# Projections of a two-layer trunk as scaled float16 pairs in place of float32r pairs

## The chip, the cores and the metric

The kernel runs on one core of one Trainium2 chip. The core has five engines that each work through their own queue in order: TensorE (PE, matmuls; its weight loads are shown as PEld), VectorE (DVE), ScalarE (ACT), GpSimd (POOL) and SyncE (SP, which issues most DMAs). The metric is the device time of one execution in microseconds (us).

## What is computed

A trunk of two layers over 2048 latent tokens and 256 context tokens, 1024 wide. The reference, cut to what matters here:

```python
def ab_layer(x, xc, mod, mod_c, w_in, w_out, ...):
    h, gate = adaln(x, mod)                 # rmsnorm(x) * (1 + scale) + shift
    hc, gate_c = adaln(xc, mod_c)
    ... = heads_ab(h @ w_in, *wts)          # splits: cq 256, ckv 256, kr 32, gq 512, gk 128, gv 128, gate 1024
    qa = (rmsnorm(cq, cq_gain) @ w_uq)      # 8 latent heads of 64 + 32
    kv = (rmsnorm(ckv, ckv_gain) @ w_ukv)
    oa = joint_dense_attention(qa, ka, va, kac, vac)
    ob = joint_dense_attention(qb, kb, vb, kbc, vbc)
    mix = concatenate([oa, ob]) * silu(g)
    x = x + gate * (mix @ w_out)            # the same for the context xc

def cd_layer(...):                          # second layer
    ... = heads_cd(h @ w_in, q_gain, k_gain)  # q 512, k 128, v 128, gb 512, gcc 512, gh 512, gate 1024
    oc = joint_window_attention(q, k, v, kc, vc, sink)
    od = gb * short_conv(gcv * gh, conv_w)
    mix = concatenate([oc, od]) * silu(g)
    x = x + gate * (mix @ w_out)
```

## The kernel before

Tokens are worked in 18 tiles of 128: two of context, sixteen of latents. A projection multiplies a tile's normalized tokens, transposed, by weights, over 8 inner blocks of 128. To be near float32, each operand is split into a high and a low part, `hh`, `hl` and `wh`, `wl`, both of type float32r: the high part is a rounding copy by ACT, the low part the difference, by DVE (weights) or POOL (tokens). `mm3` (lines 136 to 143) makes three matmuls per inner block: high by high, high by low, low by high. PE loads the token block as weights for each matmul.

The phases, with their times in the profile:
1. To about 490 us: the modulation of layer 0 is computed (`mod_first`, PE matmuls `pm` over `modw`), weights `wina` (512 columns), `winb` (800) are loaded and split; per tile `x_h` makes `hh`, `hl` (`hf` on DVE, line 244), then `pA` (512 columns), `pB` (288), `pC` (512), and from the latent parts `pq` (2 x 384, weights `wuq`) and `pk` (2 x 512, weights `wkv`); then rope and the transposes of queries and keys (line 559). The framework's scheduler sets the order here. `issue_after` places weight loads behind the modulation's loads on SP's queue.
2. To about 2195 us: attention of 16 heads, in 592 slots (U) whose order is written out by hand (`manual_schedule`, so PE, ACT, DVE and POOL run in that order). A slot has scores (lines 912, 913), exponentials, their split into a float16 pair, and the products with the values (702 to 704); a row maximum for a later block (791, 792) runs ahead. Background steps are spread over slots by `spread(list, first, last)`: `row_steps` (layer 1's modulation), the splits of `wg`, `gate_steps` (`pbg`, lines 682 to 684: per tile and half of the gate 8 steps of three matmuls), the splits of `wo`.
3. To about 2720 us: per tile `stage_a` (silu gate times attention output, transposed and split to `m`), `stage_b` (`py`, two blocks of 512 by `wo`, then residual, line 1057), `stage_c` (`x_h` of layer 1), `stage_d` (`pk` 256 columns, `pq` and `pg` 512 each, the last two for latents only). Weights `w4kv`, `w4q`, `w4g` are loaded and split at the start of this phase, the convolution's `w50` and `w51` near its end.
4. To about 3080 us: the convolution's projections `pz`, 8 blocks of 256 tokens, lines 1198 to 1200, 3072 matmuls of 256 columns.
5. To the end: window attention and the last output projection.

## Time and profile before

| | us |
|---|---|
| median of 3 runs | 3453.53 (3451.55 to 3456.27) |
| the profiled execution | 3457.61 |
| its span from first to last instruction | 3455.7 |
| PE busy | 3299.8 |
| DVE busy | 2326.8 |
| POOL busy | 2042.8 |
| ACT busy | 1752.0 |

In the profile's rows the first number is the start (timeline) or the line of the code, "out<-in" are the program's tile names, x the count. Busy time of PE counts a matmul to its modelled end, so that neighbours overlap; the distance from one start to the next is the pace. Idle time of an engine is shown with the instruction that ended it ("<-"). PEclk is the granted clock of PE as a share of full speed.

### The profile page before, as it was taken

The numbers are of one execution on the slowest core, as the hardware profiler recorded it, in microseconds if no ns is written. First come the engines' busy times: TensorE is split into PE (matmuls) and PEld (weight loads), VectorE is DVE, ScalarE is ACT, GpSimd is POOL, SyncE is SP. The second block draws the span as 40 slices with busy tenths as digits, with TensorE's granted clock in tenths as the row PEclk, the third lists the DMA queues.
The fourth block names the chain that finished last, engine by engine and source line by source line (L and its number), as shares of the span: only waits on it lengthen the run. The fifth ranks groups of instructions, "written<-read, shape, count | busy, mean of one in ns | idle before, by whom it ended". The sixth has DMA issues, their size and how long they took to land. (4 is left out here: it accounts for less than half of the span.)

```text
span 3455.7 us, 75435 instructions
## 1 busy us (share of the span) xinstructions
PE 3299.8 (95%) x30863; PEld 2393.5 (69%) x30863; DVE 2326.8 (67%) x4853; ACT 1752.0 (51%) x2425; POOL 2042.8 (59%) x1590
## 2 busy tenths in 40 slices
PE   8999979999999999999999998799999899989999
PEld 4878744555655555666666664588887899976776
DVE  6888876777777777666766668555555422268886
ACT  4656644666666666666666676422323211033443
POOL 3677745777877787777877777444443211134554
PEclk9999979999999999999999999899999999999999
DMA  6444462112121211111111121444445422253332
GB/s 253 123 135 130 121 187 84 47 48 60 38 58 44 58 53 51 41 54 50 54 38 52 50 82 31 148 136 137 148 142 175 130 65 59 72 154 93 96 104 79
DMA packets 360975, 317.89 MB, mean 92 GB/s; under 512 B 211210, under 2 KB 300122, under 8 KB 360626
## 3 DMA queue, kind: packets, MB, share of 16 engines
q1 hardware_dynamic: 356016, 300.47, 28.6%
q10 hardware_dynamic: 4612, 12.60, 1.2%
q8 instruction: 242, 3.96, 0.5%
q14 instruction: 105, 0.86, 0.1%
HBM read 196.58 MB, written 116.41 MB: 91 GB/s over the span
## 5 line engine op out<-in xcount | busy, mean ns | idle before, releaser
L898 POOL TENSOR_TENSOR Pl<-P,Ph 128x1024 f16<-128x1024 f32 (+1 forms) x592 | 1257.3, 2135 | 438.7 <-DVE Ph L895 212.6
L792 DVE TENSOR_REDUCE part<-mx 128x1 f32<-128x512 f32 x1024 | 687.8, 687 | 372.8 <-PE mx L791 366.5
L702 PE MATMUL av<-v,Ph 128*128 128x65 f16 x5296 | 629.7, 194 | 15.6 <-DVE O L937 11.6
L703 PE MATMUL av<-v,Ph 128*128 128x64 f16 x5296 | 628.8, 195 | 0.0
L704 PE MATMUL av<-v,Pl 128*128 128x65 f16 x5296 | 622.0, 193 | 6.5 <-POOL Pl L898 3.4
L702 PEld LDWEIGHTS <-Ph 128*128 128x128 f16 x5296 | 500.5, 97 | 146.6 <-issue 54.1
L703 PEld LDWEIGHTS <-Ph 128*128 128x128 f16 x5296 | 495.2, 98 | 124.3 <-issue 3.5
L912 PE MATMUL sT<-qh,k 96*128 96x512 f16 (+2 forms) x1776 | 578.2, 380 | 1.7 <-ACT P L915 1.7
L704 PEld LDWEIGHTS <-Pl 128*128 128x128 f16 x5296 | 494.7, 99 | 25.4 <-POOL Pl L1369 12.9
L915 ACT ACTIVATE P<-sT,qsca 128x1024 f32<-128x1024 f32 (+1 forms) x296 | 326.3, 1102 | 336.2 <-PE sT L913 326.6
L913 PE MATMUL sT<-q,k 100*128 100x512 f16 (+2 forms) x1184 | 450.2, 381 | 2.1 <-DVE q L808 2.0
L915 ACT ACTIVATE P<-sT,qscb 128x1024 f32<-128x1024 f32 (+1 forms) x296 | 326.5, 1103 | 247.6 <-PE sT L913 237.9
L791 PE MATMUL mx<-k,qh 96*128 96x512 f16 (+1 forms) x1024 | 396.9, 388 | 33.0 <-DVE part L792 24.9
L897 ACT CAST Ph<-P 128x1024 f16<-128x1024 f32 (+1 forms) x395 | 408.3, 1034 | 11.2
L1369 POOL TENSOR_TENSOR Pl<-P,Ph 128x512 f16<-128x512 f32 x156 | 184.5, 1200 | 157.8 <-DVE Ph L1368 67.9
L912 PEld LDWEIGHTS <-k 96*128 96x128 f16 (+1 forms) x1776 | 155.8, 99 | 111.3 <-issue 9.7
L791 PEld LDWEIGHTS <-qh 96*128 96x128 f16 (+1 forms) x1024 | 100.5, 98 | 141.7 <-issue 83.1
L913 PEld LDWEIGHTS <-k 100*128 100x128 f16 (+1 forms) x1184 | 115.1, 97 | 108.9 <-issue 6.2
L895 DVE CAST Ph<-P 128x1024 f16<-128x1024 f32 (+1 forms) x197 | 153.9, 781 | 8.2 <-ACT P L915 7.1
L1029 POOL TENSOR_TENSOR og<-og 128x1024 f32<-128x1024 f32 x18 | 44.0, 2444 | 174.6 <-ACT og L1028 174.6
L1198 PE MATMUL pz<-hx,w51wg 128*128 128x256 f32 x512 | 143.8, 281 | 0.0
L1199 PE MATMUL pz<-hx,w51wg 128*128 128x256 f32 x512 | 143.5, 280 | 0.0
(441 smaller groups left out, 7989.9 us busy)
## 6 DMA issues: line engine op xcount, KB each, us to landing
bgh<-s_hT SPq DMA_DIRECT2D x36, 512.0 KB, 5.4
xt<-in_x SPq DMA_DIRECT2D x32, 512.0 KB
roww<-in_mod_w SPq DMA_DIRECT2D x64, 256.0 KB, 2.8
hx<-s_h1T SPq DMA_DIRECT2D x32, 512.0 KB, 4.4
s_hT<-hh SPq DMA_DIRECT2D x18, 512.0 KB, 2.6
s_hT<-hl SPq DMA_DIRECT2D x18, 512.0 KB, 2.6
s_Gd<-bgg SPq DMA_DIRECT2D x36, 256.0 KB, 5.0
og<-s_Gd SPq DMA_DIRECT2D x18, 512.0 KB, 6.9
```

The source lines that it names most:

```text
L702: nc.tensor.matmul(o, Ph, v[:, 0:65], start=first, stop=False, skip_group_check=True)
L703: nc.tensor.matmul(o[:, 0:64], Ph, v[:, 66:130], start=False, stop=False, skip_group_check=True)
L704: nc.tensor.matmul(o, Pl, v[:, 0:65], start=False, stop=last, skip_group_check=True)
L791: nc.tensor.matmul(m, q["qh"][0:kk, i * 128:(i + 1) * 128], k1[0:kk, c * 512:(c + 1) * 512], start=True, stop=True)
L792: nc.vector.reduce_max(part[:, i, c:c + 1], m, axis=X)
L895: nc.vector.tensor_copy(hs, ps_)
L897: nc.scalar.copy(hs, ps_)
L898: nc.gpsimd.tensor_tensor(ls, ps_, hs, op=ALU.subtract)
L912: nc.tensor.matmul(s[:, j, :w], kk[0:rows_, ks], q["qh"][0:rows_, :w], start=pi == 0, stop=False)
L913: nc.tensor.matmul(s[:, j, :w], d["last"][0:r2, ks], q["q2"][0:r2, :w], start=False, stop=True)
L915: nc.scalar.activation(P[:, :, :w], s[:, :, :w], AF.Exp, scale=d["sc"][:, 2:3])
L1369: nc.gpsimd.tensor_tensor(Pl, P, Ph, op=ALU.subtract)
```

## The change

All projections but the last output projection take float16 pairs. So that float16's range holds, operands are scaled by powers of two: weights by one scale per weight matrix, found from the largest absolute value (`weights16`: load all rows; `top`, a maximum per row block on DVE; `fin`, which brings the maximum over the partitions by a PE transposition, makes the power of two in `pow2` and spreads it by a PE matmul; `split`, ACT then DVE); tokens by a scale from the modulation (`mod_scale`), which is multiplied into the modulation; the gated attention output by a scale per token. The results are scaled back where they are copied from PSUM, by factors from `inv2`. Raw weights now stay in buffers of their own until the scale is known. In phase 1 the load of `wina` stands ahead of the modulation's loads. In phase 2 the loads of `wg` and `wo` are at slots 1 and 44, their maxima at 8 to 18 and 54 to 64. `hT`, `h1T` and `hx` are half as large. Gate and attention output of `stage_a` are two tiles instead of one.

```diff
-        self.hT = [s(f"hT{i}", (NT, 128, D)) for i in range(2)]
+        self.hT = [s(f"hT{i}", (NT, 128, D), F16) for i in range(2)]
...
+    def pow2_bits(self, e, m, top):
+        nc = self.nc
+        nc.vector.tensor_scalar(e, m.bitcast(I32), 0x7F800000, None, op0=ALU.bitwise_and)
+        nc.vector.tensor_scalar(e, e, float(40 << 23), float(230 << 23), op0=ALU.max, op1=ALU.min)
+        nc.vector.tensor_scalar(e, e, -1.0, float((253 + top) << 23), op0=ALU.mult, op1=ALU.add)
+    def inv_bits(self, o, e):
+        self.nc.vector.tensor_scalar(o, e, -1.0, float(254 << 23), op0=ALU.mult, op1=ALU.add)
+    def pow2(self, ps, tag, m1, top, name):
+        nc, c = self.nc, self.c
+        m = c.tile([1, 1], F32, name=f"pm{name}")
+        e = c.tile([1, 2], I32, name=f"pe{name}")
+        sc = c.tile([128, 2], F32, name=f"pw{name}")
+        pt = ps.tile([128, 512], F32, tag=tag, name="pw")
+        nc.tensor.transpose(pt[0:1, 0:128], m1, self.ident)
+        nc.vector.tensor_reduce(m, pt[0:1, 0:128], axis=X, op=ALU.max)
+        self.pow2_bits(e[:, 0:1], m, top)
+        self.inv_bits(e[:, 1:2], e[:, 0:1])
+        p2 = ps.tile([128, 512], F32, tag=tag, name="pw2")
+        nc.tensor.matmul(p2[:, 0:2], self.ones1, e.bitcast(F32), start=True, stop=True)
+        nc.vector.tensor_copy(sc, p2[:, 0:2])
+        return sc
+    def weights16(self, ps, pstag, name, n, nk, src, rp, rtag, outs, scale=None, chunk=None):
+        nc, c = self.nc, self.c
+        raws, S = [], {}
+        am = c.tile([128, nk], F32, name=f"am{name}")
+        Ws = [[[], []] for _ in outs]
+        chunk = chunk or n
+        def load(k):
+            raw = rp.tile([128, n], F32, tag=f"{rtag}{k}", name=f"{name}r{k}")
+            raws.append(raw)
+            for cs, ap in src(k):
+                dst = raw[:, cs]
...
+                S["dma"] = nc.sync.dma_start(out=dst, in_=ap)
+        def top(k):
+            if scale:
+                nc.vector.tensor_scalar(raws[k], raws[k], scale(k), None, op0=ALU.mult)
+            nc.vector.tensor_reduce(am[:, k:k + 1], raws[k], axis=X, op=ALU.max, apply_absolute_value=True)
+        def fin():
+            m1 = c.tile([128, 1], F32, name=f"am1{name}")
+            nc.vector.tensor_reduce(m1, am, axis=X, op=ALU.max)
+            S["sc"] = self.pow2(ps, pstag, m1, 9, name)
+        def split(k, o, c0):
+            pool, tag, b0, w = outs[o]
+            if c0 == 0:
+                for i in range(2):
+                    Ws[o][i].append(pool.tile([128, w], F16, tag=f"{tag}{i}_{k}", name=f"{name}{o}{i}_{k}"))
+            d = slice(c0, min(w, c0 + chunk))
+            x = slice(b0 + d.start, b0 + d.stop)
+            wh, wl = Ws[o][0][k][:, d], Ws[o][1][k][:, d]
+            nc.scalar.activation(wh, raws[k][:, x], AF.Identity, scale=S["sc"][:, 0:1])
+            nc.vector.scalar_tensor_tensor(wl, raws[k][:, x], S["sc"][:, 0:1], wh, op0=ALU.mult, op1=ALU.subtract)
...
+        return loads, mids, splits, Ws, S
+    def inv2(self, name, a, b, f=None):
+        o = self.c.tile([128, 2], F32, name=f"iv{name}")
+        self.nc.vector.tensor_scalar(o[:, 0:1], a, b, None, op0=ALU.mult)
...
+        return o
+    def mod_scale(self, layer, ps, tag):
+        nc, c = self.nc, self.c
+        m = self.mod[layer]
+        am = c.tile([128, 2], F32, name=f"mam{layer}")
+        for i in range(2):
+            nc.vector.tensor_reduce(am[:, i:i + 1], m[:, i * KD:(i + 1) * KD, :].rearrange("p b j -> p (b j)"), axis=X, op=ALU.max, apply_absolute_value=True)
+        m1 = c.tile([128, 1], F32, name=f"mam1{layer}")
+        nc.vector.tensor_scalar(m1, am[:, 1:2], float(D) ** 0.5, am[:, 0:1], op0=ALU.mult, op1=ALU.add)
+        sc = self.hsc[layer] = self.pow2(ps, tag, m1, 14, f"h{layer}")
+        nc.vector.tensor_scalar(m, m, sc[:, 0:1], None, op0=ALU.mult)
...
-        hh = wp.tile([128, KD, 128], F32R, tag="hh", name="hh", bufs=bufs)
-        hl = wp.tile([128, KD, 128], F32R, tag="hl", name="hl", bufs=bufs)
+        hh = wp.tile([128, KD, 128], F16, tag="hh", name="hh", bufs=bufs)
+        hl = wp.tile([128, KD, 128], F16, tag="hl", name="hl", bufs=bufs)
...
+                la, ma, sa, (wina,), xa = self.weights16(ps, "tr", "wina", 512, KD, self.rows_of(a["ab_w_in"][0], 0, 512), wt, "ra", [(wt, "wina", 0, 512)])
+                lb, mb, sb, (winb,), xb = self.weights16(ps, "tr", "winb", NP1 - 512, KD, self.rows_of(a["ab_w_in"][0], 512, NP1 - 512), wt, "rb",
+                                                         [(wt, "winb", 0, NP1 - 512)])
+                for f in la:
+                    f()
                 self.x_norm(S[tiles[0]]["xt"], gp, sqrt=True)
-                after = self.mod_first(sp, ps, "mm")
+                with tc.issue_after(xa["dma"].ins):
+                    after = self.mod_first(sp, ps, "mm")
+                for f in ma + sa:
+                    f()
+                self.mod_scale(0, ps, "tr")
                 x_tr(tiles[0])
                 with tc.issue_after(after.ins):
-                    sa, wina = self.weights(wt, "wina", 512, KD, self.rows_of(a["ab_w_in"][0], 0, 512))
-                    sb, winb = self.weights(wt, "winb", NP1 - 512, KD, self.rows_of(a["ab_w_in"][0], 512, NP1 - 512),
-                                            sub=lambda k: (nc.vector, nc.gpsimd)[k % 2])
-                    for f in sa + sb:
+                    for f in lb + mb + sb:
                         f()
...
-                nc.scalar.copy(c, pA)
+                nc.scalar.activation(c, pA, AF.Identity, scale=iva)
...
+            lg, mg, sg, (wg,), xg = self.weights16(ps, "mx", "wg", D, KD, self.rows_of(a["ab_w_in"][0], NP1, D), wgp, "wgr", [(wgp, "wg", 0, D)], chunk=512)
+            lo, mo, so, (wo,), xo = self.weights16(ps, "mx", "wo", D, KD, self.rows_of(a["ab_w_out"][0], 0, D), wgp, "wgr", [(wgp, "wg", 0, D)], chunk=512)
             gate = self.gate_steps(sp, hp, ps, wg, 1)
-            so, wo = self.weights(wgp, "wo", D, KD, self.rows_of(a["ab_w_out"][0], 0, D), tag="wg", extra=(hp, "h1"), chunk=512)
...
-            spread([lambda f=f: behind(f) for f in sg], 15, 40)
+            spread([lambda f=f: behind(f) for f in lg], 1, 2)
+            spread(mg + [ivg], 8, 18)
...
-            spread(rows[n0 + nd:], U - 40, U - 2)
+            spread(rows[n0 + nd:], U - 44, U - 6)
+            spread([lambda: self.mod_scale(1, ps, "mx")], U - 4, U - 3)
...
+                am = wp.tile([128, 1], F32, tag="am", name="am", bufs=2)
+                nc.vector.tensor_reduce(am, g, axis=X, op=ALU.max, apply_absolute_value=True)
+                e = wp.tile([128, 2], I32, tag="ae", name="ae", bufs=3)
+                self.pow2_bits(e[:, 0:1], am, 14)
+                self.inv_bits(e[:, 1:2], e[:, 0:1])
+                nc.scalar.activation(g, g, AF.Identity, scale=e.bitcast(F32)[:, 0:1])
+                m = hp.tile([128, 2, KD, 128], F16, tag="h1", name="m")
...
-                    nc.vector.tensor_tensor(x1[:, cs], py, g[:, cs], op=ALU.mult)
+                    nc.vector.scalar_tensor_tensor(x1[:, cs], py, iv, g[:, cs], op0=ALU.mult, op1=ALU.mult)
...
+            todo = []
             for nm, c0, w in (("kv", 512, 256), ("q", 0, 512), ("g", 2304, 512)):
-                ss, W[nm] = self.weights(kvp if nm == "kv" else w4, f"w4{nm}", w, KD, self.rows_of(a["cd_w_in"][0], c0, w), extra=(wp, "sq"))
-                for f in ss:
...
+            for x in todo:
+                for f in x[1]:
                     f()
+            IV = {}
+            for nm, _, mids, splits, (W[nm],), x in todo:
+                for f in mids + splits:
+                    f()
+                IV[nm] = self.inv2(nm, x["sc"][:, 1:2], self.hsc[1][:, 1:2], 0.125)
...
+                    c0 = self.conv_weights(ps, 0, ((1, 2), (0, 3)), wgp, [(w4, "w4q", 0, 512), (w4, "w4g", 512, 512)])
+                    for f in c0[0] + c0[1] + c0[2]:
+                        f()
             self.v_scales(wp, ps)
-            c1, W1 = self.conv_weights(1, (0, 1, 2, 3), wgp, "wg", (wp, "xt"))
-            for f in c1:
+            c1 = self.conv_weights(ps, 1, ((0, 1, 2, 3),), wgp, [(wgp, "wg", 0, D)])
+            for f in c1[0] + c1[1] + c1[2]:
...
-                nc.vector.tensor_tensor(u[:, 2:B + 2], pz[1], tmp, op=ALU.mult)
+                iv = self.ivc[c // 2]
+                nc.scalar.activation(tmp, pz[0], AF.Identity, scale=iv)
+                nc.vector.scalar_tensor_tensor(u[:, 2:B + 2], pz[1], iv, tmp, op0=ALU.mult, op1=ALU.mult)
```

Where the change moves instructions, the engines' queues stand as follows (line numbers of after are those of the changed program).

DVE, phase 1, before the first tile's `hf`. `winar`, `wkvr` and so on are raw weights, `macc` the modulation, `am` maxima, `pe` and `pw` the steps of a scale. Before:

```order
L108 TENSOR_TENSOR wina_5_276<-winar_274,wina_5_275 128x512
L196 TENSOR_TENSOR macc<-macc,pm 2x512
L108 TENSOR_TENSOR wina_6_282<-winar_280,wina_6_281 128x512
L108 TENSOR_TENSOR winb_0_294<-winbr_292,winb_0_293 128x800
L199 COPY mod_73<-prt 128x32
L597 MEMSET von 10x128
L108 TENSOR_TENSOR wina_7_288<-winar_286,wina_7_287 128x512
L244 TENSOR_SCALAR hf<-pt,mod_73 128x128 x8
```

After, the place at which the scale of `wina` is made (its last two steps and copy; the splits of `wina` and then `hf` follow):

```order
L136 TENSOR_SCALAR pewina<-pewina 1x1
L181 TENSOR_REDUCE amwuq<-wuqr_412 128x1
L220 TENSOR_SCALAR mam_295<-mam_292 128x1
L180 TENSOR_SCALAR wkvr_446<-wkvr_446,gcmla_ckv_gain 128x1024
L181 TENSOR_REDUCE amwuq<-wuqr_414 128x1
L137 TENSOR_SCALAR pewina<-pewina 1x1
L180 TENSOR_SCALAR wkvr_448<-wkvr_448,gcmla_ckv_gain 128x1024
L181 TENSOR_REDUCE amwkv<-wkvr_446 128x1
L185 TENSOR_REDUCE am1wuq<-amwuq 128x1
L141 TENSOR_SCALAR pewina<-pewina 1x1
L181 TENSOR_REDUCE amwkv<-wkvr_448 128x1
L156 COPY pwwina<-pw_257 128x2
```

The splits of `wina` stood between the steps of the modulation; now the steps of its scale stand between the scalings and maxima of `wuq` and `wkv`.

PE, the start of phase 1, `prt` the modulation's transposition, `pw` a scale's. Before:

```order
L191 MATMUL pm<-modw,sc 2x512 x32
L198 MATMUL prt<-ident,macc 128x2 x4
L241 MATMUL pt<-ident,xt 128x128 x8
L198 MATMUL prt<-ident,macc 128x2 x12
L241 MATMUL pt<-ident,xt 128x128 x8
L141 MATMUL pA<-wina_0_245,hh 128x512
L142 MATMUL pA<-wina_0_246,hh 128x512
```

After:

```order
L286 MATMUL pm<-modw,sc 2x512 x32
L293 MATMUL prt<-ident,macc 128x2 x4
L150 MATMUL pw<-ident,am1wina 1x128
L293 MATMUL prt<-ident,macc 128x2 x12
L155 MATMUL pw_257<-pewina,ones_72 128x2
L150 MATMUL pw<-ident,mam_295 1x128
L155 MATMUL pw_307<-peh_298,ones_72 128x2
L336 MATMUL pt<-ident,xt 128x128 x8
L150 MATMUL pw<-ident,am1winb 1x128
L233 LDWEIGHTS hh
L233 MATMUL pA<-wina_0_260,hh 128x512
```

Transpositions of `xt` and the first `pA` now stand behind the two scales' transpositions and matmuls.

DVE, the start of phase 3, up to the first product of the output projection (`x<-py`). Before:

```order
L108 TENSOR_TENSOR w4kv_0_34371<-w4kvr_34369,w4kv_0_34370 128x256
L108 TENSOR_TENSOR w4kv_1_34377<-w4kvr_34375,w4kv_1_34376 128x256
L108 TENSOR_TENSOR w4kv_2_34383<-w4kvr_34381,w4kv_2_34382 128x256
L1057 TENSOR_TENSOR x_34275<-py,gbc 128x512
L108 TENSOR_TENSOR w4kv_3_34389<-w4kvr_34387,w4kv_3_34388 128x256
L1058 TENSOR_TENSOR x_34275<-x_34275,xt 128x512
```

After:

```order
L181 TENSOR_REDUCE amw4g<-w4gr_34602 128x1
L181 TENSOR_REDUCE amw4g<-w4gr_34604 128x1
L185 TENSOR_REDUCE am1w4kv<-amw4kv 128x1
L181 TENSOR_REDUCE amw4g<-w4gr_34606 128x1
L181 TENSOR_REDUCE amw4g<-w4gr_34608 128x1
L181 TENSOR_REDUCE amw4g<-w4gr_34610 128x1
L181 TENSOR_REDUCE amw4g<-w4gr_34612 128x1
L181 TENSOR_REDUCE amw4g<-w4gr_34614 128x1
L1143 TENSOR_REDUCE am<-gg 128x1
L181 TENSOR_REDUCE amw4g<-w4gr_34616 128x1
L135 TENSOR_SCALAR ae<-am 128x1
L1177 SCALAR_TENSOR_TENSOR x_34464<-py,ivt,gbc 128x512
```

Three splits of `w4kv` stood ahead of that product; now the maxima of `w4kv` and `w4g` do, and the splits come behind it.

More of the change, by code (lines that the diff above doesn't have):

```diff
@@ L71, in __init__ @@
         self.x1d = s("x1d", (SEQ, D))
-        self.h1T = [s(f"h1T{i}", (NT, 128, D)) for i in range(2)]
+        self.h1T = [s(f"h1T{i}", (NT, 128, D), F16) for i in range(2)]
         self.QT1 = [s(f"QT1{i}", (8 * 64, TOK), F16) for i in range(2)]
@@ new lines, in weights16 @@
+    def weights16(self, ps, pstag, name, n, nk, src, rp, rtag, outs, scale=None, chunk=None):
[9 more added lines that the diff above has]
+                dst = raw[:, cs]
+                if len(ap.shape) == 3:
+                    dst = dst.rearrange("p (s c) -> p s c", s=ap.shape[1])
+                S["dma"] = nc.sync.dma_start(out=dst, in_=ap)
[17 more added lines that the diff above has]
+            nc.vector.scalar_tensor_tensor(wl, raws[k][:, x], S["sc"][:, 0:1], wh, op0=ALU.mult, op1=ALU.subtract)
+        loads = [lambda k=k: load(k) for k in range(nk)]
+        mids = [lambda k=k: top(k) for k in range(nk)] + [fin]
+        splits = [lambda k=k, o=o, c0=c0: split(k, o, c0) for k in range(nk) for o in range(len(outs)) for c0 in range(0, outs[o][3], chunk)]
+        return loads, mids, splits, Ws, S
@@ L1008, in gate_bcast, with phase34 @@
         return out
-    def phase34(self, wo, wgp, hp, w4, tiles=range(NT)):
+    def phase34(self, wo, xo, wgp, hp, w4, tiles=range(NT)):
         nc, tc, a = self.nc, self.tc, self.a
@@ L1147, in phase34 @@
-            for f in c1:
-                f()
-            self.wconv = {(0, s): (W, x) for (_, W), p in zip(pairs, ((1, 2), (0, 3))) for x, s in enumerate(p)}
-            self.wconv.update({(1, s): (W1, s) for s in range(4)})
-    def conv_weights(self, cp, parts, pool, tag, extra=None):
-        runs = {(1, 2): ((0, 2, 1280),), (0, 3): ((0, 1, 768), (1, 1, 2816)), (0, 1, 2, 3): ((0, 3, 768), (3, 1, 2816))}[parts]
+            c1 = self.conv_weights(ps, 1, ((0, 1, 2, 3),), wgp, [(wgp, "wg", 0, D)])
@@ new lines, in phase34, with conv_weights @@
+            for f in c1[0] + c1[1] + c1[2]:
+                f()
+            self.wconv = {(0, s): (W, x) for W, p in zip(c0[3], ((1, 2), (0, 3))) for x, s in enumerate(p)}
+            self.wconv.update({(1, s): (c1[3][0], s) for s in range(4)})
+            self.ivc = [self.inv2(f"c{i}", x[4]["sc"][:, 1:2], self.hsc[1][:, 1:2])[:, 0:1] for i, x in enumerate((c0, c1))]
+    def conv_weights(self, ps, cp, groups, rp, outs):
+        base = (768, 1280, 1792, 2816)
+        order = [p for g in groups for p in g]
@@ L1157, in src @@
         def src(k):
             rows = self.a["cd_w_in"][0, k * 128:(k + 1) * 128, :]
-            return [(slice(x * 256, (x + m) * 256), rows[:, c0:c0 + 512 * m].rearrange("p (s c) -> p s c", c=512)[:, :, cp * 256:cp * 256 + 256])
-                    for x, m, c0 in runs]
-        return self.weights(pool, f"w5{cp}{tag}", 256 * len(parts), KD, src, tag=tag, extra=extra)
+            return [(slice(x * 256, (x + 1) * 256), rows[:, base[p] + cp * 256:base[p] + cp * 256 + 256]) for x, p in enumerate(order)]
@@ L1164, in hx_load @@
+        return self.weights16(ps, "tr", f"w5{cp}", 256 * len(order), KD, src, rp, "wgr", outs, chunk=512)
     def hx_load(self, pool, b):
-        hx = [pool.tile([128, KD, 2, 128], F32R, tag=f"h{i}", name=f"hx{i}", bufs=1) for i in range(2)]
+        hx = [pool.tile([128, KD, 2, 128], F16, tag=f"h{2 + i}", name=f"hx{i}", bufs=1) for i in range(2)]
         for j in range(2):
@@ L1506, in emit @@
         if 3 in phases:
-            P.phase34(wo, wgp, hp, w4)
+            P.phase34(wo, xo, wgp, hp, w4)
         if 4 in phases:
```

101 lines of the change are left out of this document (56 added, 45 removed).

## The prediction

> **What bounds the kernel now.** I read the busy lines of the page first, then busy time in chosen stretches, then the spacing of matmuls in the timeline.
>
> ```profile
> PE 3299.8 (95%) x30863; PEld 2393.5 (69%) x30863; DVE 2326.8 (67%) x4853; ACT 1752.0 (51%) x2425; POOL 2042.8 (59%) x1590
> PE   8999979999999999999999998799999899989999
> DVE  6888876777777777666766668555555422268886
> core 0: us, PE busy (x) PEld busy (x) DVE busy (x) ACT busy (x) POOL busy (x), PEclk, DMA share, GB/s
> 200.00:300.00 100.00, 95.30 (x590) 80.59 (x588) 88.50 (x203) 61.42 (x156) 71.81 (x118) 1.00 0.45 132
> ...
> 600.00:700.00 100.00, 91.23 (x1056) 54.88 (x1055) 76.78 (x120) 63.49 (x67) 70.82 (x34) 0.94 0.16 43
> 1500.00:1700.00 200.00, 199.74 (x2406) 128.87 (x2403) 131.25 (x221) 136.19 (x131) 155.26 (x75) 1.00 0.16 49
> 2100.00:2200.00 100.00, 79.67 (x1003) 49.27 (x1000) 60.92 (x95) 61.09 (x66) 71.43 (x33) 0.90 0.10 29
> 2200.00:2300.00 100.00, 91.88 (x448) 75.06 (x447) 63.91 (x177) 37.70 (x69) 37.38 (x42) 0.93 0.55 193
> 2300.00:2400.00 100.00, 100.00 (x520) 83.28 (x519) 55.40 (x164) 28.16 (x52) 49.53 (x64) 1.00 0.40 138
> ...
> 2800.00:2900.00 100.00, 100.00 (x845) 100.00 (x845) 22.57 (x61) 10.02 (x26) 10.24 (x17) 1.00 0.32 87
> ```
>
> TensorE (PE) carries the time: 95% busy, and 100 of 100 us in the output projections (2300 to 2400) and the convolution's projections (2800 to 2900), nearly that in the attention (1500 to 1700). There a matmul that takes its turn sooner is time won, one for one. In phase 1 (200 to 300) DVE is only 7 us behind PE, so DVE caps what a faster PE wins. At the joints (2100 to 2300) PE already waits.
>
> **What a float16 matmul is worth.** Busy time overlaps, so I take start-to-start distances: float32r 512 columns (pq), float16 512 (scores) and float16 256, 512 and 384 of the window stage, then float32r 256 (pz).
>
> ```profile
> 2269.42 0.40 PE L143 MATMUL pq<-w4q,hl 128*128 128x512 f32 x1
> ...
> 2271.06 0.39 PE L141 MATMUL pq<-w4q,hh 128*128 128x512 f32 x1
> 1502.24 0.38 PE L912 MATMUL sT<-qh,k 128*128 128x512 f16 x1
> ...
> 1503.11 0.38 PE L791 MATMUL mx<-k,qh 128*128 128x512 f16 x1
> 3149.34 0.38 PE L1306 MATMUL pc<-k,qT 128*128 128x256 f16 x2
> 3149.56 0.32 PE L1311 MATMUL pl<-k,qT 128*128 128x384 f16 x1
> 3149.72 0.38 PE L1355 MATMUL sT<-qT,k 128*128 128x512 f16 x1
> 2849.79 0.28 PE L1198 MATMUL pz<-hx,w50w4g 128*128 128x256 f32 x1
> ...
> 2850.38 0.28 PE L1200 MATMUL pz<-hx,w50w4g 128*128 128x256 f32 x1
> ```
>
> Seven float32r steps of 512 take 1.64 us, .2343 each; four float16 steps take .87, .2175 each: .0168 won per matmul. Five float32r steps of 256 take .59, .118 each; the float16 pair takes .22, .110 each: .008 won, or .009 if half of .2175 holds (.1088). Every one of these has a weight load of its own.
>
> In the attention, a projection step of three float32r matmuls stands alone between float16 ones:
>
> ```profile
> 1500.86 0.48 PE L682 MATMUL pbg<-wg,bgh 128*128 128x512 f32 x1
> 1501.17 0.40 PE L683 MATMUL pbg<-wg,bgh 128*128 128x512 f32 x1
> 1501.41 0.40 PE L684 MATMUL pbg<-wg,bgh 128*128 128x512 f32 x1
> 1501.65 0.39 PE L791 MATMUL mx<-k,qh 128*128 128x512 f16 x1
> L682 PE MATMUL pbg<-wg,bgh 128*128 128x512 f32 x288 | 139.3, 484 | 0.0
> L682 PEld LDWEIGHTS pbg<-wg,bgh 128*128 128x128 f32 x288 | 54.8, 190 | 2.1
> L702 PEld LDWEIGHTS <-Ph 128*128 128x128 f16 x5296 | 500.5, 97 | 146.6 <-issue 54.1 <-DVE O L937 19.8 <-DVE Ph L1368 4.4
> ```
>
> It holds PE for .79 us; its first matmul is .07 longer, since a float32 load takes 190 ns and stands behind short matmuls, where a float16 load takes 97. Three float16 matmuls would take .65: .14 won, 288 times.
>
> The page "TensorE: Matmul & The Clock Gate" of the Trainium skill, section "Back-to-back issue gap", gives about 216 ns for an isolated warm 512-column matmul and 131 ns sustained for pairs of load and matmul. The scores' .2175 are such pairs and agree with the first, not the second; what the second would make of the time is the last rival below.
>
> **Gains.** Each count is tiles times column blocks times 8 inner blocks times 3.
> - Gate steps, attention: 288 x .137 = **39 us**, PE-bound there. Without the load effect 864 x .0168 = 15.
> - Phase 3: out projection 18 x 2 x 24 = 864, pq and pg 16 x 2 x 24 = 768, at .0168: 27; pk 432 x .0085 = 4. Minus what the joints don't bind on, **29**.
> - Convolution: 3072 x .0085 = **26** (25 to 28).
> - Phase 1: per tile 60 matmuls of 512 and 36 shorter ones. At the .229 spaced in that stage for pA (below) .0115 x 60 = .7, the 36 others about .4: 1.1 per tile; 16 steady tiles 18 us if PE alone bound. But DVE has 88.5 of each 100 us with work that stays, and PE's own wait is on a chain through ACT:
>
> ```profile
> 187.56 0.51 PE L559 MATMUL pt<-ident,mqh 128*128 128x128 f16 x6 [1.18 <-ACT mqh L547]
> ...
> 307.43 0.51 PE L559 MATMUL pt<-ident,mqh 128*128 128x128 f16 x6 [1.18 <-ACT mqh L547]
> 47.44 0.40 PE L141 MATMUL pA<-wina,hh 128*128 128x512 f32 x1
> ...
> 49.73 0.39 PE L142 MATMUL pA<-wina,hh 128*128 128x512 f32 x1
> ```
>
> Five tiles in 119.87 us, 23.97 each, of it 21.2 for DVE. pA: ten steps in 2.29, .229 each. I take **14** (0 to 20).
>
> Sum 39 + 29 + 26 + 14 = 108.
>
> **What it adds.** At the start the weights' scale must be known before any weight can be split. Before: modulation matmuls from 8.48, then the first pA; DMA feeds the weights behind them.
>
> ```profile
> 8.48 30.56 PE L191 MATMUL pm<-modw,sc 128*2 128x512 f32 x64 [2.88 <-DMA modw<-in_mod_w]
> 24.11 7.83 SPq L126 DMA_DIRECT2D winar<-in_ab_w_in  x8
> 32.26 5.00 ACT L107 CAST wina<-winar 128x512 fp32r<-128x512 f32 x8 [22.49 <-DMA winar<-in_ab_w_in]
> 40.71 0.97 DVE L108 TENSOR_TENSOR winb<-winbr,winb 128x800 fp32r<-128x800 f32 x1
> 42.40 2.62 DVE L244 TENSOR_SCALAR hf<-pt,mod 128x128 f32<-128x128 f32 x8
> 44.45 0.50 PE L141 MATMUL pA<-wina,hh 128*128 128x512 f32 x1
> 69.81 0.39 PE L143 MATMUL pA<-wina,hl 128*128 128x512 f32 x1
> L529 DVE TENSOR_REDUCE v<-sq 128x8 f32<-128x768 f32 x18 | 16.9, 941 | 0.0
> L106 DVE TENSOR_SCALAR wkvr<-wkvr,gcmla_ckv_gain 128x1024 f32<-128x1024 f32 x2 | 2.1, 1051 | 1.2 <-DMA wkvr<-in_mla_w_ukv 1.2
> ```
>
> Now the load of wina (2.1 MB) is issued ahead of the modulation's, so modulation ends some 5 us later, about 44 (8 pieces took 7.8 us to issue). On DVE the small steps of wina's scale stand behind eight maxima of winb (800 wide, .97 by the winb row), four scalings and four maxima of wuq and wkv (.94 to 1.05) and the DMA waits of these: some 16 us of DVE work, and wkv's pieces are the last loads. I put wina's scale at 58 in place of the first cast at 32; then 5 us of casts (the ACT row), whose first piece frees PE, and hf's 2.6 us after the modulation is rescaled: first pA near 65 instead of 44.45. winb's splits again follow their scale, on PE's queue behind pA: 8 x .97 on ACT and DVE. I walked this to the end of tile 1's pA: 88 against 69.81. **Loss 19.** Lower bound 5 (the load alone), upper 26. Phase 1 has no later slack that returns it.
>
> Attention: eight maxima 1024 wide of wg (slots 8 to 18) and of wo (54 to 64). From L529's 941 at 768 I estimate 1.2 us each, 20 us on a DVE with 76.8 of 100 us taken (600 to 700); maxima of the scores queue behind them and PE waits for those. The slots of the two batches last some 60 us, with 14 free: 6 lost. Each scale is a transposition, a maximum, four small steps and a matmul in PE's order, about 2 us in which PE stands at its matmul unless work lies between; wg, wo and the second layer's modulation: 3 us. Late loads of w4q, whose maxima stand in DVE's order by the last slots, behind buffers that wo's splits free: 2. **Loss 11** (3 to 20).
>
> Start of phase 3: eight maxima each for kv and g (.4 to .7) are in DVE's order ahead of the first product of the out projection, and kv, q and g split only after their scales: PE runs out of PSUM tiles and then waits for pk's weights. DVE has about 8 us more, plus three chains of some 2. **Loss 8** (3 to 14). The per-token scale of each tile (a 1024 maximum, four small steps, an ACT pass) lies beside PE's 100 of 100 us, DVE being at 55.4: nothing, at most 1 us a tile if it came late (18). Convolution: c1's loads, eight maxima (9.6 us) and splits start only behind the last tile, but its weights are needed after c0's work, so a loss of 3 (0 to 8). Smaller stores of hT and h1T are hidden: DMA share is .32 to .40.
>
> Losses 19 + 11 + 8 + 3 = 41. Net **-67**. The profiled execution took 3457.61 us (span 3455.7 and 1.9 around it), 4.1 over the median 3453.53; less 67 it gives 3390.6, and from the median 3386.5. I say **3388**.
>
> The same page, section "What's actually happening", has PE drop to half clock after about 3.4 us idle. The profile shows a granted clock of .93 in 2200 to 2300, where PE waits; a start with PE idle from 44 to 65 would by that rule cost some 2 us more, which the bound of 26 holds.
>
> **Rivals.**
> 1. *Small costs.* Chains hide beside other work and start-up costs 10: losses 5 to 15, net -93 to -103, 3350 to 3361. For it: ACT and DVE idle at the joints. Against: in-order queues.
> 2. *DVE becomes the bound.* Phase 1 wins nothing (-14) and the maxima cost their upper ends (26, 20, 14, 8): 94 - 68 = 26 won, 3427. For it: 88.5 in phase 1. Against: each upper end has slack before it.
> 3. *Matmuls aren't faster.* If what makes .234 of .2175 isn't the type but, say, a full 128-row weight in a row of three, only the gate steps' load gap goes: 288 x .07 = 20 won, 41 lost, 21 **slower**: 3475. It decides at the spacing: some 4,900 matmuls of 512 columns in all (256 counted half), so losses outweigh from 21 / 4900 = .0043 won, a float16 spacing above .230. Against: L1355 has 128 x 128 weights in float16 and takes .22.
> 4. *A large stall* that I don't see, at one joint: by a DVE wait for a load that waits for a buffer PE frees. 108 us would have to be lost for no gain, 67 more than I count; against: all idle time of PE, over the whole span, is 156 us today (3455.7 less 3299.8).
> 5. *Closer rows.* If consecutive float16 matmuls overlapped, each hundredth of a us below .2175 would win 49 us more on 4,900 of them; at half of .2175, some 530, about 2860. Against: the spacing of the scores, .2175 over four steps, and of L1355, .22. By the 131 ns of the Trainium skill's page it would be about 2960; no row of the trace bears that out.
>
> **Chances.** Forecast (net -45 to -93) 0.70; small costs 0.09; DVE bound 0.11; not faster 0.06; a large stall 0.03; closer rows 0.01. The range for 8 in 10: 3345 to 3435, with both bounds of the joints. Faster by over 0.2% (7 us, about what a measurement of this kernel can tell from no change) 0.89; within it 0.03; slower 0.08 (the third rival and most of the fourth).
>
> **What would show it.** Starts of consecutive pz matmuls .109 apart and of pq .2175; gate steps .65; first pA near 65 and pA of tile 1 done near 88; phase 1 at about 23.1 a tile; PE waiting for DVE in slots 8 to 18 and 54 to 64 and before the first pk. I am wrong if float16 spacing here exceeds .225, or if PE idle time grows by over 60 us.

## The result, and the profile after

| | before | after |
|---|---|---|
| median, runs side by side (us) | 3454.84 (3451.55 to 3456.27) | 3432.36 (3430.84 to 3434.76) |
| span of the profiled execution (us) | 3455.7 | 3433.0 |
| ratio after / before, 95% interval | | 0.9937 (0.992 to 0.9954) |

About 22 us faster, where 67 were forecast. The page of after, PE's busy time and the two rows of tenths that show its work and its granted clock in 40 slices:

```profile
PE 3205.5 (93%) x30902; PEld 2012.4 (59%) x30902; DVE 2448.2 (71%) x5158; ACT 1811.1 (53%) x2451; POOL 2018.3 (59%) x1586
PE   6999968899999999999999998689999799989999
PEclk8999988999999999999999999889999899989999
```

PE's busy time fell by 94.3 us (from 3299.8), the span by 22.7. So PE stands more: 227.5 us without work instead of 155.9. Busy time in the stretches that were shown of before:

```profile
core 0: us, PE busy (x) PEld busy (x) DVE busy (x) ACT busy (x) POOL busy (x), PEclk, DMA share, GB/s
200.00:300.00 100.00, 92.41 (x605) 53.69 (x604) 86.63 (x204) 68.14 (x162) 76.21 (x123) 1.00 0.41 110
600.00:700.00 100.00, 82.31 (x962) 49.15 (x963) 79.22 (x125) 59.55 (x64) 64.47 (x31) 0.95 0.25 71
2200.00:2300.00 100.00, 72.15 (x347) 38.38 (x348) 76.87 (x220) 37.31 (x60) 26.79 (x27) 0.80 0.55 177
2300.00:2400.00 100.00, 100.00 (x574) 55.28 (x572) 72.45 (x201) 38.56 (x64) 46.52 (x63) 1.00 0.40 135
2800.00:2900.00 100.00, 100.00 (x918) 89.63 (x916) 25.15 (x67) 13.06 (x29) 11.60 (x19) 1.00 0.20 46
```

The steady stages stay full of PE work and hold more matmuls in 100 us (574 for 520, 918 for 845). The joint at 2200 went from 91.88 to 72.15, and its granted clock from .93 to .80. The pace of the float16 pairs, from the timeline of after: the output projection, the convolution, and a gate step between its neighbours.

```profile
2307.67 0.38 PE L233 MATMUL py<-wo,m 128*128 128x512 f16 x1
...
2311.34 0.38 PE L235 MATMUL py<-wo,m 128*128 128x512 f16 x1
2829.81 0.27 PE L1328 MATMUL pz<-hx,w 128*128 128x256 f16 x1
...
2830.90 0.27 PE L1329 MATMUL pz<-hx,w 128*128 128x256 f16 x1
1500.49 0.38 PE L786 MATMUL pbg<-wg,bgh 128*128 128x512 f16 x1
...
1501.14 0.38 PE L895 MATMUL mx<-k,qh 128*128 128x512 f16 x1
```

17 steps in 3.67 us are .216 each (the scores of before gave .2175), ten of 256 columns in 1.09 are .109, and the gate step is .65. All three are as forecast. Where the two timelines drift apart, by the starts of the same instruction in both, in order of the program (minus: after gains on before; the two profiled spans differ by the sum):

| stretch | forecast | measured |
|---|---|---|
| start, to pA of tile 3 | +19 | +21.9 |
| phase 1 on, to pA of tile 17 | -14 | -10.3 |
| end of phase 1, to the scores of slot 0 | 0 | +6.2 |
| slots 0 to 66 | with the next but one +11 | +18.4 |
| slots 66 to 550 (gate steps) | -39 | -33.1 |
| slots 550 to 591 | see above | +4.9 |
| to py of tile 2 (start of phase 3) | +8 | +19.0 |
| py of tile 2 to tile 16 | -29 | -27.0 |
| to pz no. 385 (start of the convolution) | +3 | -2.3 |
| pz no. 385 to the last | -26 | -24.6 |
| to the end | 0 | +4.1 |
| sum | -67 | -22.8 |

(Of the forecast's 29 and 26, two tiles and 384 pz lie in the row "to pz no. 385"; at the pace of their neighbours these win 3.9 and 3.5, so about 5 are lost at that joint.) With them the gains are 102 of the 108 forecast, and the losses 80 instead of 41.

### The profile page after: what moved, and what is told of

It is laid out like the page before. It is cut to its first block, busy times and chain, and to the rows that moved or that the text cites. A ratio compares the mean times of both kernels' runs of the same rounds, so it can differ in the third digit from the quotient of the medians.

```text
span 3433.0 us, 75844 instructions
## 1 busy us (share of the span) xinstructions
PE 3205.5 (93%) x30902; PEld 2012.4 (59%) x30902; DVE 2448.2 (71%) x5158; ACT 1811.1 (53%) x2451; POOL 2018.3 (59%) x1586
## 5 line engine op out<-in xcount | busy, mean ns | idle before, releaser
L1009 ACT CAST Ph<-P 128x1024 f16<-128x1024 f32 (+1 forms) x395 | 407.8, 1032 | 11.3
L1330 PE MATMUL pz<-hx,w 128*128 128x256 f16 x1024 | 278.8, 273 | 5.3 <-DVE w L197 5.0
L1328 PE MATMUL pz<-hx,w 128*128 128x256 f16 x1024 | 279.0, 273 | 1.0 <-ACT tmp L1343 0.9
L1329 PE MATMUL pz<-hx,w 128*128 128x256 f16 x1024 | 278.9, 273 | 0.0
```

The source lines that it names most:

```text
L1009: nc.scalar.copy(hs, ps_)
L1328: nc.tensor.matmul(p[:, 0:B], wh[k][:, cs], hv, start=k == 0, stop=False)
L1329: nc.tensor.matmul(p[:, 0:B], wh[k][:, cs], lv, start=False, stop=False)
```

## The experiments

Two theories at first. A: the losses are the price of finding the scales (maxima, the chain to a power of two and back, waits behind them in in-order queues). B: they are something else of the change, such as later loads, splits of two passes or a joint that a faster PE merely waits at. Four kernels put constants in place of scales, first by phase, then all at once. In this diff the names listed are those of the group; the modulation's and the token's scale are replaced likewise. Powers of two that suit the data are built in, so these kernels show times and are no replacement.

```diff
+            if name not in FIX:
+                nc.vector.tensor_reduce(am[:, k:k + 1], raws[k], axis=X, op=ALU.max, apply_absolute_value=True)
...
+            if name in FIX:
+                S["sc"] = self.fx[FIX[name]]
+                return
```

**Constants in phase 1** (`wina`, `winb`, `wuq`, `wkv`, the modulation of layer 0).

> Leaves out, in phase 1 alone, the finding of scales (maxima, transpositions, power-of-two steps of wina, winb, wuq, wkv and of layer 0's modulation); constants stand in their place, all else is the changed kernel. Theory A (the price is the finding of scales in in-order queues): the first pA starts near 50 us instead of 62.9, pA of tile 1 near 68 instead of 88.1, and the kernel is 14 to 20 us faster than the changed one: 3412 to 3418. Theory B (phase 1 is bound by DVE, ACT and POOL together, so an earlier start is given back by its end): less than 8 us faster, 3424 to 3432, with the first scores of the attention at 525 to 532 instead of 531.8.

3416.26 us, ratio 0.9895 (0.9879 to 0.9911): 16 us under after. At pA of tile 3 the loss is 5.8 instead of 21.9. The first pA is at 54.6 (near 50 was expected), still 10.2 later than before. That part is not the finding of scales; the load of `wina` ahead of the modulation's and the order of the work around it are left for it, and were not taken apart.

**Constants in the attention** (`wg`, `wo`, the modulation of layer 1).

> Leaves out the finding of the scales of wg, wo and of layer 1's modulation in the attention; constants stand in their place. The changed kernel lost 18.9 us against the one before between slots 12 and 66 and 4.7 in the last four slots. Theory A: these come from the maxima and the chains, so 18 to 24 us faster than the changed kernel: 3408 to 3414. Theory B (the splits by ACT and DVE at slots 20 to 40, now reading three operands, are what costs): the loss at slots 12 to 54 stays, some 6 us, and the gain is 11 to 14: 3418 to 3421.

3413.48 us, 0.9884 (0.987 to 0.9899): 19 us under after. Between slots 0 and 66 the kernel loses 1.4 instead of 18.4, and between 550 and 591 nothing.

**Constants in phases 3 and 4** (`w4kv`, `w4q`, `w4g`, `w50`, `w51`, and the scale per token).

> Leaves out the finding of the scales of w4kv, w4q, w4g, w50, w51 and of the per-token scale of the gated attention output (maximum and power of two; the scaling pass of ScalarE stays); constants stand in their place. Theory A: the 19 us lost at the start of phase 3 fall to 5 to 9 and the 6 at the convolution's start to 0 to 3, so 13 to 20 us faster than the changed kernel: 3412 to 3419. Theory B (the order of the loads and the splits, not the scales, sets the start of phase 3): under 6 us faster, 3426 to 3432.

3398.80 us, 0.9849 (0.9833 to 0.9866): 33.6 us under after, more than either theory had. From slot 591 to py of tile 2 it wins 5.9 where after loses 19.0, and some 9 more come at the start of the convolution.

**All constants.**

> All three together: every scale but the last projection's is a constant, so what is left is float16 pairs with splits, scaling passes and rescaling on the way out of PSUM. Theory A: the parts add, 50 to 64 us faster than the changed kernel: 3368 to 3382, some 75 to 85 under the kernel before. Theory B: 15 to 30 us faster, 3402 to 3417.

3364.61 us, 0.9742 (0.9728 to 0.9757): 67.8 us under after; the three parts (16.1, 18.9, 33.6) add to 68.6. So the price of finding scales is about 68 us, spread over separate places, and what is left, the float16 pairs with their splits and scaling passes, wins 89 (3453.27 less 3364.61 in the same runs). Some losses stay: 5.3 to pA of tile 3, 3.6 in the last stage, and 5.9 between the last pC and slot 0. PE's waits at this last place, by groups (line, operation, busy time and mean, then the idle time ahead of them), of before:

```profile
L372 PE MATMUL pt<-ident,gqh 128*128 128x128 f16 x16 | 1.8, 262 | 7.3 <-ACT gqh L358 5.0 <-DVE gqh L359 2.2
L141 PE MATMUL pq<-wuq,ch 128*128 128x384 f32 x4 | 1.4, 362 | 1.4 <-ACT ch L499 1.4
```

and of after:

```profile
L233 PE MATMUL pk<-wkv,ch 128*128 128x512 f16 x4 | 2.0, 506 | 0.0
L467 PE MATMUL pt<-ident,gqh 128*128 128x128 f16 x16 | 1.8, 263 | 9.5 <-ACT gqh L453 7.3 <-DVE gqh L454 2.2
L233 PE MATMUL pq<-wuq,ch 128*128 128x384 f16 x4 | 1.7, 422 | 4.2 <-ACT ch L603 4.2
```

PE is done sooner and waits 5.0 us longer for the same passes of ACT (2.8 for `ch`, 2.3 for `gqh`, by these rows). It then runs the first pk at half clock: four from 483.13 on start .425 apart, which brings the mean of that row to 506 ns where before has 392 to 396. I read this as phase 1's gain handed back in part at its end; the loss is there with and without scales, but no run shows that the earlier end is its cause.

**Order alone.** Two moves: `wina`'s maxima, scale and splits ahead of the modulation in the program; `wo`'s maxima spread over slots 300 to 500 instead of 54 to 64.

```diff
+                for f in ma + sa:
+                    f()
                 with tc.issue_after(xa["dma"].ins):
                     after = self.mod_first(sp, ps, "mm")
-                for f in ma + sa:
-                    f()
...
-            spread(mo, 54, 64)
+            spread(mo, 300, 500)
```

> Two moves, nothing left out. (1) Maxima, scale and splits of wina stand in the program ahead of the modulation's matmuls, so that on PE the scale's transposition and matmul come before the 64 modulation matmuls instead of behind them. Theory A (wina's scale was late since its steps stood behind the modulation on PE and behind winb, wuq and wkv on DVE): first pA 8 us earlier, near 55, as with constants (54.6), and pA of tile 3 near 120 instead of 131.9. Theory B (winb's scale and splits and the token path set the start anyway): first pA earlier, but pA of tile 3 within 3 us of 131.9. (2) The maxima and scale of wo at slots 300 to 500 instead of 54 to 64. Theory A (eight maxima of 1.2 us stand in DVE's order where DVE has no time left): of the 12.7 us lost between slots 54 and 66 at least 9 are won, and little is lost at slots 300 to 500, where DVE is 66 to 70% busy. Theory B (the scale's chain, in which PE waits, is the price): 3 us or less are won. Both A: 3408 to 3414; both B: 3427 to 3432.

3415.08 us, 0.9894 (0.9879 to 0.9909): 17 us under after. Two thirds of it are `wo`: slots 54 to 66 win 2.0 instead of losing 12.5, and after the maxima at their new place 11.3 of the 14.5 are left at slot 591. Most of the rest is the start (pA of tile 3 at 127.3 instead of 131.9). Slots 54 to 66 of before, of the changed kernel, of the kernel further down that has only the token's scale as a constant (its code up to here is the changed kernel's), and of this one (PE busy, PEld, DVE, ACT, POOL, then the granted clock):

```profile
695.80:732.00 36.20, 34.28 (x402) 20.57 (x399) 29.60 (x48) 21.68 (x21) 25.94 (x13) 0.95 0.19 47
719.40:768.20 48.80, 41.38 (x406) 23.05 (x403) 38.74 (x63) 21.71 (x21) 25.71 (x13) 0.83 0.14 35
720.40:763.10 42.70, 33.83 (x406) 19.91 (x403) 38.94 (x63) 21.72 (x21) 25.39 (x13) 1.00 0.16 40
714.30:748.50 34.20, 32.28 (x402) 19.39 (x399) 29.49 (x48) 21.70 (x21) 25.90 (x13) 1.00 0.20 50
```

Two things add up here. DVE has some 39 us to do with the maxima and 29.5 without, and before took 36.2 for these slots: the work doesn't fit, as theory A of the expectation has it. In the third row DVE has no more than 3.8 us free. So 6.5 of the 12.5 are lost at full clock, 2.4 of them at the chain's two steps on PE (1.22 and 1.16). The other 6 came in the changed kernel's profile with a granted clock of .83. They aren't in the code: the third row has the same 406 matmuls and 63 DVE instructions at 1.00. The profile with constants in phase 1 has 42.7 at 1.00 too, two others (constants in phases 3 and 4, and for the `w4` weights) 46.7 at .89. A single profile's loss in this stretch is thus uncertain by 6 us.

Slots 8 to 15, where `wg`'s maxima stand, of before:

```profile
545.90:576.00 30.10, 29.33 (x260) 12.78 (x257) 17.20 (x32) 11.77 (x11) 14.32 (x7) 1.00 0.44 134
```

DVE is busy for 17.2 of 30.1 us there, so `wg`'s maxima had room.

The start was a miss: first pA at 60.3 where the expectation had 55. PE there in this kernel, and in the changed one:

```profile
52.77 0.37 PE L150 MATMUL pw<-ident,mam 128*1 128x128 f32 x1 [5.28 <-DVE mam L220]
56.52 0.58 PE L155 MATMUL pw<-peh,ones 1*128 1x2 f32 x2 [3.39 <-DVE peh L141]
...
60.26 0.61 PE L233 MATMUL pA<-wina,hh 128*128 128x512 f16 x1 [1.04 <-ACT hh L341]
```

```profile
54.58 0.58 PE L155 MATMUL pw<-pewina,ones 1*128 1x2 f32 x2 [8.56 <-DVE pewina L141]
...
57.46 0.55 PE L155 MATMUL pw<-peh,ones 1*128 1x2 f32 x2 [1.99 <-DVE peh L141]
...
62.94 0.61 PE L233 MATMUL pA<-wina,hh 128*128 128x512 f16 x1 [2.82 <-ACT hh L341]
```

The 8.56 us for `wina`'s scale are gone, and 5.28 and 3.39 for the modulation's scale stand in their place, since its steps are in DVE's order behind the maxima of `winb`, `wuq` and `wkv`.

**The scale in steps.** As above, and `fin` of `wg` and `wo` cut into five background steps (maximum, transposition, power of two, matmul, copy) that stand in different slots, so that each has its operand when its turn comes. `wg`'s steps also use the PSUM bank of the gate steps.

```diff
-            spread(mg + [ivg], 8, 18)
-            spread(sg, 20, 40)
+            spread(mg[:KD], 8, 15)
+            spread(mg[KD:] + [ivg], 15, 21)
+            spread(sg, 21, 41)
...
```

> As e5_order, and the scales of wg and wo are made in five background steps of consecutive slots (maximum over the columns, transposition, power of two, spreading matmul, copy) instead of in one, wg's over the bank of the gate steps, whose first use comes later. Theory A (PE stands 3.15 and 1.07 us at wg's scale because each step of the chain waits for the one before on another engine, and runs at half clock afterwards): the 6 us lost at slots 12 to 18 fall to 1 to 2, 3404 to 3410. Theory B (DVE's eight maxima of wg there are the price): they stay at 4 to 6, within 2 us of e5_order.

3414.34 us, 0.9888 (0.9872 to 0.9905). Slots 15 to 18 lose 0.2 instead of 6.1; the time misses the 3404 to 3410 that were expected with it. Up to the last pz the kernel is 5.5 ahead of the one before, but its profiled execution loses 3.4 more than that one in the last stage, and the medians differ by 0.7; I can't say why. PE at `wg`'s scale in the changed kernel:

```profile
601.13 0.33 PE L150 MATMUL pw<-ident,am1wg 128*1 128x128 f32 x1 [3.15 <-DVE am1wg L185]
602.54 0.58 PE L155 MATMUL pw<-pewg,ones 1*128 1x2 f32 x2 [1.07 <-DVE pewg L141]
...
604.13 1.04 PE L1024 MATMUL sT<-qh,k 96*128 96x512 f16 x2
604.97 0.63 PE L1025 MATMUL sT<-q,k 100*128 100x512 f16 x1
605.39 1.06 PE L1024 MATMUL sT<-qh,k 96*128 96x512 f16 x2
...
608.67 0.59 PE L1024 MATMUL sT<-qh,k 96*128 96x512 f16 x2
609.10 0.38 PE L1025 MATMUL sT<-q,k 100*128 100x512 f16 x1
609.32 0.60 PE L1024 MATMUL sT<-qh,k 96*128 96x512 f16 x2
```

4.2 us of standing: the transposition waits 3.15 for a maximum that is in DVE's order behind the scores' maxima, the next step 1.07. Then three score matmuls take 1.26 us (604.13 to 605.39) where at 608.67 they take .65: half clock for some 4 us, another 2 lost. That is the 6.1. The eight maxima of `wg` in slots 8 to 15 cost nothing that shows: slots 0 to 15 are 0.5 us shorter than before.

**The scale per token as a constant; the scales of `w4kv`, `w4q`, `w4g` as constants.** Two kernels for the start of phase 3.

> The changed kernel with the per-token scale alone a constant (maximum and power of two of the gated attention output left out, the scaling pass stays). Theory A (at the start of phase 3 the maximum, four small steps and the scaling pass of the first two tiles are a chain that PE waits out, 7.2 and 4.7 us before the transpositions): the delay from the last scores of the attention to py of tile 2, 104.0 us before the change against 85.7 with nothing but later scales constant, falls by 6 to 10 us from the changed kernel's value. Theory B (only the weights' scales count there): 2 us or less. On the later tiles nothing, 25.64 us each.

(This one misquotes the stretch from slot 591 to py of tile 2: that is 66.7 us before, 85.7 in the changed kernel and 60.8 with all constants of phases 3 and 4.)

> The changed kernel with the scales of w4kv, w4q and w4g alone constants. Theory A (their maxima and three chains, with splits only behind them, hold up pk and pq of the first tile): the same stretch at the start of phase 3 falls by 12 to 17 us. Theory B (the token scale is the main price): 6 us or less.

3420.25 us, 0.9908 (0.9889 to 0.9928), and 3426.46 us, 0.9926 (0.9906 to 0.9946). The stretch loses 10.0 and 8.9 instead of 19.0: 9.0 and 10.1 back. (Of the second, 12 to 17 or under 6 were expected; it is neither.) Both together, with those of the convolution's weights, brought 24.9, so about 6 of it show only when neither is there to wait for, or belong to `w50`, whose maxima start in this stretch; which of these wasn't taken apart. DVE, ACT and PE there in the changed kernel (from the timeline, PE's rows apart):

```profile
2217.69 2.81 DVE L181 TENSOR_REDUCE amw4g<-w4gr 128x1 f32<-128x512 f32 x4 [1.28 <-DMA w4gr<-in_cd_w_in]
2221.87 1.22 DVE L1143 TENSOR_REDUCE am<-gg 128x1 f32<-128x1024 f32 x1 [1.37 <-POOL gg L1141]
...
2236.32 1.22 DVE L1143 TENSOR_REDUCE am<-gg 128x1 f32<-128x1024 f32 x1 [3.83 <-POOL gg L1141]
2237.45 0.15 DVE L156 COPY pww4kv<-pw 128x2 f32<-128x2 f32 x1
```

```profile
2207.00 1.15 ACT L1147 ACTIVATE gg<-gg,ae 128x1024 f32<-128x1024 f32 x1 [10.88 <-DVE ae L137]
...
2225.29 1.15 ACT L1147 ACTIVATE gg<-gg,ae 128x1024 f32<-128x1024 f32 x1 [5.87 <-DVE ae L137]
...
2237.64 3.30 ACT L196 ACTIVATE w4kv<-w4kvr,pww4kv 128x256 f16<-128x256 f32 x8 [3.78 <-DVE pww4kv L156]
```

```profile
2208.20 1.97 PE L1154 MATMUL pt<-ident,gg 128*128 128x128 f32 x8 [7.17 <-ACT gg L1147]
2226.49 1.97 PE L1154 MATMUL pt<-ident,gg 128*128 128x128 f32 x8 [4.67 <-ACT gg L1147]
...
2252.82 0.40 PE L233 MATMUL pk<-w4kv,hh 128*128 128x256 f16 x1 [4.89 <-ACT hh L341]
```

Two chains block each other. PE waits for the scaled gate `gg`, ACT for the token's scale, DVE's maximum of the token for POOL's product: three hand-overs, where before PE took POOL's product itself. And `w4kv`'s scale is late twice: its matmul stood in PE's order behind products of py until 2235.05, though DVE's step for it was ready at 2230.65, and its copy at 2237.45 stands in DVE's order behind the maximum of a third tile, which waited 3.83 us for POOL. ACT's splits start only then (2237.64), and since they take 13.3 us, with one other pass between them, `hh` for the first pk comes at 2252.

**The start in another order, and layer 1's modulation scale in steps.** On top of the scale in steps: loads of `wina` behind the first loads of the modulation, those of `wuq` and `wkv` behind the first tile's store, `winb`'s scale ahead of the modulation's; near slot 591 the modulation's rows end earlier and its scale stands in six background steps.

```diff
-            spread(rows[n0 + nd:], U - 44, U - 6)
-            spread([lambda: self.mod_scale(1, ps, "mx")], U - 4, U - 3)
+            spread(rows[n0 + nd:], U - 52, U - 14)
+            spread(self.mod_steps(1, ps, "mx"), U - 13, U - 6)
...
```

> As e6_order_steps, with three more moves, nothing left out. (1) The loads of wina stand behind the first four of the modulation's sixteen, not ahead of all: the modulation's matmuls start near 8.5 us again and end near 39 to 40. (2) The loads of wuq and wkv are issued behind the first tile's store, and winb's scale ahead of the modulation's, so that on DVE the modulation's scale no longer stands behind the scaling and maxima of wuq and wkv, and winb is split before the first pA ends. Theory A (in e5 the start was held by these: PE waited 5.3 and 3.4 us for steps of the modulation's scale that stood behind them on DVE, then for winb's splits): pA of tile 3 near 112 to 117 instead of 127, start and phase 1 some 10 to 14 us better. Theory B (the token path through DVE, ACT and POOL sets the pace of the first tiles): under 5 us better. (3) Layer 1's modulation scale in six background steps, ended before slot 586: of 4.7 us lost in the last slots, at least 2 are won. A: 3398 to 3404 in all; B: 3407 to 3412.

3405.29 us, 0.9856 (0.984 to 0.9871). The end of the attention is settled: slots 550 to 591 win 1.9 instead of losing 4.9. With a constant scale, and the modulation's rows where the change has them, the loss was gone too, so the chain was the price there, not late loads. The start gave only 2 us (pA of tile 3 at 124.6; 112 to 117 were expected). PE there, then ACT:

```profile
47.18 0.37 PE L150 MATMUL pw<-ident,am1winb 128*1 128x128 f32 x1 [4.42 <-DVE am1winb L185]
...
51.59 0.58 PE L155 MATMUL pw<-peh,ones 1*128 1x2 f32 x2 [2.08 <-DVE peh L141]
52.10 1.97 PE L396 MATMUL pt<-ident,xt 128*128 128x128 f32 x8
59.49 0.61 PE L287 MATMUL pA<-wina,hh 128*128 128x512 f16 x1 [5.41 <-ACT hh L401]
```

```profile
49.44 6.93 ACT L198 ACTIVATE winb<-winbr,pwwinb 128x800 f16<-128x800 f32 x8 [23.66 <-DVE pwwinb L156]
57.77 1.06 ACT L378 ACTIVATE jx<-xt 128x1024 f16<-128x1024 f32 x1 [1.40 <-DMA xt<-in_x]
...
58.83 1.18 ACT L401 CAST hh<-hf 128x512 f16<-128x512 f32 x2
```

Now the last wait is for `hh`, which is in ACT's order behind 6.9 us of `winb`'s casts and then behind a pass over another `xt` that waited 1.40 us for its load. Each wait that I took away at the start left the next one nearly as late.

**One scale for `w4kv`, `w4q` and `w4g`**, and the convolution's first maxima and scale early in phase 3 (splits where they were); then the same with `w4g`'s scale apart again.

```diff
+            for x in todo:
+                for f in x[2][:KD]:
+                    f()
...
+            sc3 = self.pow2(ps, "tr", m3, 9, "w4")
...
-                if i == n - NC_T:
+                if i == 3:
...
```

> As e9_start_steps, and w4kv, w4q and w4g share one scale (one chain in place of three, behind all their maxima), and the maxima and scale of w50 are emitted early in phase 3. Theory A (each of three chains in PE's order costs a wait of some 2 to 3 us): 4 to 8 us better than e9. Theory B (the last load, w4g, sets the shared scale, so what is won on chains is lost on pk's later start): within 2 us of e9 or slower.

> As e10_joint_scale, but w4g keeps a scale of its own and only w4kv and w4q share one, so that pk and pq don't wait for w4g's load. Theory A of e10 (chains count): 1 to 2 us slower than e10. Theory B (the last load counts): 3 to 6 us faster than e10.

3398.29 us, 0.9835 (0.9817 to 0.9852), and 3403.30 us, 0.985 (0.9834 to 0.9865). The first is the best version that computes what it should: 57 us under its before (3455.41 in the same runs). Against the kernel ahead of it, the start of phase 3 is 2.5 better and the stretch from py of tile 16 to pz no. 385 4.4. The second is 5.0 slower by the medians (4.4 by the spans); the intervals of the ratios overlap, but each of its four runs is slower than each of the first's. 3.3 of it lie at the start of phase 3, where it has one chain more. The expectation had it 1 to 2 us slower or 3 to 6 faster: neither holds, and a cause isn't shown.

## Why the prediction failed

**Right: the price of a matmul.** Float16 at the scores' pace, the gate step at .65 and pz at .109 were read from before and came out as read. Phase 3 wins 1.93 us per tile (27.57 to 25.65), the convolution .0092 per pz. Phase 1's pace is 23.07 per tile where 23.1 was named; before has 23.81 over the same tiles, so .74 each are won. That DVE caps it isn't shown: from pA of tile 3 to that of tile 17 it is busy for 277.6 of 323 us, and of 22.5 us that PE waits there, 17.9 are for ACT's `mqh`. The 131 ns of the page "TensorE: Matmul & The Clock Gate" of the Trainium skill, section "Back-to-back issue gap", appear nowhere: 17 steps in 3.67 us are .216, which is the warm 216 ns of that section. All in all 102 of 108 were won; 33.1 of 39 at the gate steps is most of the gap, and why isn't shown. (The 4,900 matmuls of the third and fifth rivals leave out the 864 of the gate steps; the forecast doesn't use that figure.)

**Near in its sum, not in its steps: the start.** 21.9 for 19, first pA at 62.9 for 65. But the walk went to the end of tile 1's pA, 88 against 69.81. In after 88 is where this tile's pA begins:

```profile
88.08 0.61 PE L233 MATMUL pA<-wina,hh 128*128 128x512 f16 x1 [4.55 <-ACT hh L341]
...
96.91 0.38 PE L235 MATMUL pA<-wina,hl 128*128 128x512 f16 x1
```

So the walk came out 9 us short, 27 were lost by then, and 5 of them are back by tile 3: that the sum is near is in part luck. 16 of the 21.9 is finding scales (constants took these away); the other 6 were not taken apart.

**Wrong: "about 2 us in which PE stands at its matmul", 3 us in sum for three chains.** This is the main failed step. `wg`'s chain measured 6.1, the modulation's with its place at the end of the attention 4.9 (2.4 to 4.9 in the profiles of the kernels that keep it); cut into steps they cost 0.2 and nothing. I counted the chain's own instructions. Two things were missing: each step is in DVE's order behind work of another kind, so its wait is that queue's backlog, and the half clock after 4.2 us of standing.

**Wrong in the same part: "14 free: 6 lost" for the two batches of maxima.** It took one free time for both, from a stretch with DVE at 76.8 of 100 us. But DVE was busy for 17.2 of 30.1 us where the first batch went and for 29.6 of 36.2 where the second did: the first cost nothing, the second, with the chain at its end, 6.5 at full clock and 12.5 in the profiled execution. So the forecast's 6 was about right at full clock; half clock, which it had at nothing in the attention, was the rest. Attention lost 23 in all, 11 were forecast (20 at most).

**Wrong: the start of phase 3, 8 forecast (14 at most), 19.0 measured.** The step that failed is the one that puts the token's scale at nothing because it "lies beside PE's 100 of 100 us". That holds in the steady tiles, which win 27.0 with and without it, but not in the first ones, where no older tile covers it: a constant there gives 9.0 back. And the forecast's "three chains of some 2" were again priced without what stands ahead of them: constants for the three `w4` weights give 10.1 back. At the convolution the forecast of 3 was about 5 in the ledger.

**Wrong by leaving out: 0 for the joint behind phase 1 (6.2) and for the last stage (4.1).** The first is there without any scale too; as I read it, a gain of PE ends at the next wait for another engine. The last stage's code is unchanged; it loses 2.6 to 6.4 in every one of the eleven kernels. By the starts of the first 20 scores of its window attention 3.6 of after's 4.1 are there; what they are stays open.

Of the 44 us between forecast and result, 6 are smaller gains, 12 attention, 11 the start of phase 3, 10 the two joints that were left out, 3 the start, 2 the convolution. The second rival (DVE becomes the bound, 3427) came near in time, and its four losses add up to 68 where those four places lost 69. But phase 1 did win, and DVE was the bound only in a place such as slots 54 to 66: it has 71% of the span, and with constants, which also free DVE, it is at the waits and not at the steady stages that the time comes back. Of the prediction's two signs of being wrong, the float16 spacing stayed under .225, and PE's idle time grew by 71.6 us, over the 60 named.
